# Attention on one core: the next head's context keys projected in the second unit of a head instead of the first, and one PSUM bank for all projection groups

## The chip, the cores and the metric

The kernel runs on one core of a Trainium2 chip. The metric is device time in microseconds (us) of one execution, the median of several runs. TensorE (PE in the profile, its weight loads PEld) multiplies, VectorE (DVE), ScalarE (ACT) and GpSimd (POOL) do the elementwise work, and every transfer is issued from one queue, SyncE's (SP).

## The reference, cut to what matters

Two trunk layers over 1024 latent tokens and 256 context tokens of width 1024. Layer 0 has differential attention with 8 heads, layer 1 a state-space mixer; an MLP follows each. The change touches layer 0's attention alone:

```python
def diff_attention(h_lat, h_ctx, w_qkv, ...):
    q_l, k_l, v_l = split(h_lat @ w_qkv)           # 8 heads, two 64-wide components each
    q_l, k_l = rope(q_l) * scale, rope(k_l)
    k_c, v_c = split(h_ctx @ w_qkv[:, QK_COLS:])   # context keys: no rotary
    k_all, v_all = concat([k_c, k_l]), concat([v_c, v_l])      # 256 + 1024 tokens
    def attend(q, k, v):
        p = softmax(q @ k.T)                       # one softmax for each component
        w = p[:, :, 0] - lam * p[:, :, 1]
        return rmsnorm(w @ v, subln_g) * (1 - lambda_init)
```

The context's own queries attend to the 256 context keys, the latent queries to all 1280.

## The kernel before, in words

The attention is the loop over `n` at the end of `phase_b`. A head `h` has nine units. Unit 0 takes the two query tiles of the context (256 keys), units 1 to 8 one latent query tile of 128 each (1280 keys). In a unit, `scores` multiplies queries with keys into PSUM (line 516 in unit 0, line 522 later), `maxima` has DVE copy the scores out with their row extremes (lines 531 and 535), `exps` has ACT exponentiate (lines 542 and 545), and `combine` has DVE subtract the two softmaxes (lines 553 to 556). A unit's result is transposed in the next unit: `w_part` has TensorE transpose it in up to three parts (line 568; 563 for unit 0's result, which has one part) into bank 5, a half of bank 6, or bank 7, and `w_evac` brings it to SBUF as a high and a low part: the first part through ACT and DVE (lines 576 and 577), the others through ACT and POOL (lines 581 to 583). In the units that have an output to make (`pv`; unit 2 for the context pair, units 4, 6, 8 and the next head's unit 1 for the latent pairs), `values` multiplies these with the value rows into bank 6, and `pair_out` copies the sum out (line 664). Where an output of latent tokens is due, both evacuations of the parts 0 and 1 stand behind `combine`.

Each product of a projection or of `values` is three matmuls, high by high, high by low, low by high (`mm3`, lines 132 to 134).

Between this work the projections of the next head's keys and queries are spread: `proj_group(h + 1, T, g, ...)`, with `T` 1 for keys and 0 for queries, and `g` 2 for the 256 context tokens, 0 and 1 for the halves of the latent tokens. A group is eight products, 24 matmuls. The groups of the latent tokens end in `evac` (ACT line 468, DVE line 469, four small DMAs that swap halves), `sine` (POOL line 474), `add` (DVE line 477) and `store` (ACT line 137, DVE line 138 into the buffer `stg`, then the DMAs Kd<-R or Qd<-R to DRAM). The context group of the keys has no rotary: `direct` (ACT line 463, DVE line 464) writes `stg` at once, and two DMAs Kd<-R take it out. There is one `stg`. The steps after the first are queued in `post` and taken one at a time by `next_post`, two a unit.

The table `AHEAD` gives the groups of each unit. In unit 0 there are two: the keys' context group (1, 2) in bank 4, all of it right behind `scores`, and the keys' first half (1, 0) in bank 7, in three pieces between the transposes. Units 2, 3, 5 and 7 have one group each, in bank 7; the others have none. Scores take banks 0 to 4 (0 and 1 in unit 0).

The loop stands in a manual schedule, so PE, DVE, ACT and POOL run in the order in which the code is written. SP's queue isn't part of it: a scheduler places the transfers, and SP issues them strictly one after the other, so a transfer that waits holds up those behind it. The names in the order's rows: R_111 is the buffer of weights, queries, values and `stg`, R_1826 the keys, F_1827 the scores, W weights and tables, FC the rotary buffers, Kd, Qd, Vd, od, on and rsd lie in DRAM.

Of the kernel before, what the change touches and what calls it, by code (L numbers as in the profile page):

```python
# [70 lines left out]
class Prog:  # L71
# [64 lines left out]
    def split(self, hi, lo, src, lo_eng=None):  # L136
        self.nc.scalar.activation(hi, src, AF.Copy)  # L137
        (lo_eng or self.nc.vector).tensor_tensor(lo, src, hi.bitcast(F32), ALU.subtract)  # L138
# [301 lines left out]

        return split

    def proj_group(self, h, T, g, wt, bank=None):

        nc = self.nc
        n, c0 = self.G_TOK[g], (256, 768, 0)[g]
        b = (self.qb.next() if bank is None else bank)[:, 0:n]
        scale = 1.0 if T else -0.125
        t = slice(c0 - 256, c0 + 256)
        hT = self.hT[g]  # L450
        q, sw, qc, s = self.rq, self.rs, self.rc, self.stg[:, :, 0:n]

        def product(k):
            return lambda: self.mm3(b, wt[k][0], wt[k][1], hT[0][:, k], hT[1][:, k], k == 0, k == 7)

        def out():
            dst = self.Kd if T else self.Qd
            for c in range(2):
                self.dma(dst[h % 2, c, :, c0 : c0 + n].rearrange("(l r) n -> r l n", l=2),
                         s[64 * c : 64 * c + 64].bitcast(F32))  # L460

        def direct():
            nc.scalar.activation(s[:, 0], b, AF.Copy, scale=scale)
            nc.vector.scalar_tensor_tensor(s[:, 1], b, scale, s[:, 0].bitcast(F32), ALU.mult, ALU.subtract)
            out()

        def evac():
            nc.scalar.activation(q, b, AF.Copy, scale=scale)
            nc.vector.scalar_tensor_tensor(qc, b, scale, self.cosT[:, t], ALU.mult, ALU.mult)
            for j in range(4):  # L470
                self.dma(sw[32 * j : 32 * j + 32], q[32 * (j ^ 1) : 32 * (j ^ 1) + 32])

        def sine():
            nc.gpsimd.tensor_tensor(sw, sw, self.sinT[:, t], ALU.mult)

        def add():
            nc.vector.tensor_tensor(qc, qc, sw, ALU.add)

        def store():
            self.split(s[:, 0], s[:, 1], qc)  # L480
            out()

        return [product(k) for k in range(8)], [direct] if g == 2 else [evac, None, sine, add, store]
# [103 lines left out]
        return self.tc.manual_schedule(engines={nc.tensor.engine, nc.vector.engine, nc.scalar.engine, nc.gpsimd.engine})  # L587


    AHEAD = {0: ((1, 2), (1, 0)), 2: ((1, 1),), 3: ((0, 2),), 5: ((0, 0),), 7: ((0, 1),)}  # L590

    def b_start(self):

# [25 lines left out]
    def phase_b(self):  # L619
# [14 lines left out]
        def load_k(h, c):  # L634
            K = loaded[h, "k", c] = self.rv(0, 1280) if (h, c) == (7, 1) else Kr.next()
            for k0, k1 in ((0, 256), (256, 1280)):
                self.dma(K[:, k0:k1].bitcast(F32), self.Kd[h % 2, c, :, k0:k1])

        def load_v(h):
            V = loaded[h, "v"] = Vr.next(), Vr.next()  # L640
            for j in range(2):
                self.dma(V[j].bitcast(F32), self.Vd[h, j])

        def load_q(h, pair):
            Q = Qr.next()
            cols = slice(256 * pair, 256 * pair + 256)
            self.dma(Q[:, :, 0].bitcast(F32), self.Qd[h % 2, :, :, cols].rearrange("c r n -> r c n"))
            for hl in range(2):
                self.dma(Q[64 * hl : 64 * hl + 64, :, 1].bitcast(F32),
                         self.Qd[h % 2, :, 64 - 64 * hl : 128 - 64 * hl, cols].rearrange("c r n -> r c n"))  # L650
            loaded[h, pair] = Q
# [122 lines left out]
        def wo_group(i):  # L774
            g = 2 if i > 7 else i // 4
            c0 = 128 * (i - self.G_TILES[g][0])
            b = self.bank(i - 6 if 6 < i < 8 else 7)

            def product(k):
                hh, hl = (t[:, k, c0 : c0 + 128] for t in self.oT[g])  # L780
                return lambda: self.mm3(b, hh, hl, wt6[k][0], wt6[k][1], k == 0, k == 5)

            def out():
                wsum = wsums.next()
                nc.scalar.activation(wsum, b, AF.Copy)
                self.dma(self.wod[i], wsum)

            return [product(k) for k in range(6)], [out]
# [13 lines left out]
        wts = {1: split(1)}  # L802

        def next_post():
            f = post.pop(0) if post else None
            if f:
                f()
# [3 lines left out]
        def evac():  # L811
            while ready:
                self.w_evac(*ready.pop(0))

        with self.manual():
            for n in range(72 + 5):
                h, u = units[n] if n < 72 else (8, 9)
                front = n < 72
                groups = []
# [7 lines left out]
                if front:  # L827
                    K = loaded[h, 'k', 0], loaded[h, 'k', 1]
                    pair = (u + 1) // 2
                    Q = loaded[h, pair]  # L830
                    s0 = hst[:, 0, h]
                    p, sn, sm = (p0.next(), p1), self.stat.next(), self.stat.next()
                    if u == 5 and h < 7:
                        load_v(h + 1)
                        load_k(h + 1, 0)
                    if u % 2 == 0 and u < 8 and (h, pair + 1) not in loaded:
                        load_q(h, pair + 1)
                    if h < 7:
                        groups = [self.proj_group(h + 1, *a, wts[a[0]], self.bank(4) if a == (1, 2) else None)
                                  for a in self.AHEAD.get(u, ())]  # L840
                    self.scores(u, Q, K)
                    if len(groups) == 2:
                        for f in groups[0][0]:
                            f()
                    if u == 8 and h < 7:
                        load_k(h + 1, 1)
                        load_q(h + 1, 0)
                        load_q(h + 1, 1)
                    self.maxima(u, p, sm)
                    if len(groups) == 2:  # L850
                        groups[0][1][0]()
                if front:
                    if h < 7:
                        if u == 0:
# [3 lines left out]
                if 65 <= n < 75:  # L858
                    groups = [wo_group(wo_order[n - 65])]
                fills = [[], [], []]  # L860
                if h >= 7 and groups:
                    fills = [groups[0][0][i : i + 2] for i in (0, 2, 4)]
                elif groups:
                    fills = [groups[-1][0][i:j] for i, j in (((0, 4), (4, 8), (8, 8)) if u == 3 else ((0, 3), (3, 6), (6, 8)))]
                if pv:
                    values(*pv)
                for part in range(3):
                    if part < parts:
                        tb = pb[:, 256:512] if part == 1 else self.bank(7 if part == 2 and not groups else 5)
                        t = self.w_part(prev[1], prev[2], part, tb)  # L870
                        ready.append((*t, part == 0))
                    if not late or part == 2:
                        evac()
                    if part == 1:
                        next_post()
                    if front and part < 2:
                        self.exps(u, part, p, sm, s0, sn)
                    if front and part == 1:
                        if n - 7 >= 9 and (n - 7) % 9 < 5 and (n - 7) // 9 < 7:
                            norm_pair((n - 7) // 9 - 1, (n - 7) % 9)  # L880
                        self.combine(u, p, s0, sn)
                    if late and part == 1:
                        evac()
                    if part == 0:
                        todo7, run7 = run7, []
                        for f in todo7:
                            f.pop(0)()
                            if f:
                                run7.append(f)
                    if part == (2 if n < 73 else 0):  # L890
                        while sums and sums[0][0] <= n:
                            sums.pop(0)[1]()
                    for f in fills[part]:
                        f()
                if pv:
                    pair_out(*pv)
                    sums.append((n + 1, lambda a=pv: pair_sums(*a)))
                    if pv[0] == 7:
                        tail.append((n + 1, pv[1]))
                next_post()  # L900
                if groups:
                    rest = groups[-1][1]
                    rest[0]()
                    post += rest[1:]
                if h < 7 and u in (0, 2):
# [1564 lines left out]
```

## Time and profile before

| | |
|---|---|
| median of 3 runs | 2883.9 us (2876.67 to 2889.97) |
| profiled execution, its own time | 2889.5 us |
| its span, first to last instruction | 2887.7 us |
| mean granted TensorE clock | 0.985 |
| busy share of the span: PE, PEld, DVE, ACT, POOL | 95%, 79%, 70%, 47%, 35% |
| attention loop | about 220 to 866 us of the span; PE busy 605.29 of 646.00 us |
| a head | about 80 us (unit 0 of heads 2 and 3 starts at 371.46 and 451.20 us) |

A row of the timeline has start, duration, engine, line, operation, what it writes and reads, shapes and count; in brackets stands how long the engine was idle before it and what ended that. A row of the chain of waits' table has who waited for whom, the sum in us, the number of waits and the longest. Heads are counted from 0 to 7; head 7 has no next head and no projection groups.

### The profile page before, as it was taken

To read this page: it belongs to the slowest core of one execution; us is meant where nothing else is said; L and a number is where in the kernel's file an instruction comes from. 1 tells how busy PE (TensorE), PEld (TensorE's weight loads), DVE (VectorE), ACT (ScalarE), POOL (GpSimd) and SP (SyncE) were. 2 spreads that over 40 slices of the span, in tenths; PEclk is the share of its full clock that TensorE was granted. 3 is DMA by queue.
4 is the path that set the end of the run, shared out by engine and by line. 5 is a ranking of instruction groups with operands and counts; after the bars stand their busy time and mean duration, and the time that the engine had idled before them with its cause. 6 is when DMAs were issued, how large, how long until landed. Compare 5 with 4: busy or idle time off the path is not lost. (4 is left out here: it accounts for less than half of the span.)

```text
span 2887.7 us, 43592 instructions
## 1 busy us (share of the span) xinstructions
PE 2738.5 (95%) x15225; PEld 2288.3 (79%) x15225; DVE 2009.4 (70%) x2968; ACT 1361.9 (47%) x2551; POOL 1016.2 (35%) x899
## 2 busy tenths in 40 slices
PE   6999999999999999999999999789899999999999
PEld 4687888888877888778877778688788777888887
DVE  5456788778873676666788768799533597768466
ACT  3425555555654743323444435477443633344443
POOL 3314666666663600000020003588120243336314
PEclk9999999999999999999999999899899999999999
DMA  9955555555736458886799887479843144467544
GB/s 299 306 172 168 152 173 170 171 163 165 252 98 185 123 197 311 280 298 214 261 292 294 263 251 246 155 230 279 261 135 106 63 162 164 157 222 245 164 131 142
DMA packets 447785, 586.33 MB, mean 203 GB/s; under 512 B 60494, under 2 KB 293196, under 8 KB 444364
## 3 DMA queue, kind: packets, MB, share of 16 engines
q1 hardware_dynamic: 447564, 583.53, 63.6%
q8 instruction: 120, 1.97, 0.3%
q14 instruction: 101, 0.83, 0.1%
HBM read 396.38 MB, written 182.82 MB: 201 GB/s over the span
## 5 line engine op out<-in xcount | busy, mean ns | idle before, releaser
L132 PE MATMUL PS<-H 128*128 128x512 f32 x1056 | 415.7, 395 | 7.5 <-DVE FD L1622 5.0
L134 PE MATMUL PS<-H 128*128 128x512 f32 x1056 | 412.6, 391 | 3.1 <-DVE H L138 1.6
L133 PE MATMUL PS<-H 128*128 128x512 f32 x1056 | 413.8, 392 | 0.0
L132 PE MATMUL PS<-H,R 128*128 128x512 f32 (+1 forms) x828 | 308.8, 375 | 4.7 <-DVE FU L1545 1.7
L133 PE MATMUL PS<-H,R 128*128 128x512 f32 (+1 forms) x828 | 299.7, 362 | 1.4 <-POOL H L138 1.4
L134 PE MATMUL PS<-H,R 128*128 128x512 f32 (+1 forms) x828 | 298.9, 362 | 0.0
L132 PEld LDWEIGHTS PS<-H 128*128 128x128 f32 x1056 | 199.1, 189 | 54.1 <-DVE FD L1622 4.9
L134 PEld LDWEIGHTS PS<-H 128*128 128x128 f32 x1056 | 199.2, 189 | 46.5 <-DVE H L138 2.6
L133 PEld LDWEIGHTS PS<-H 128*128 128x128 f32 x1056 | 199.2, 189 | 40.9 <-issue 1.0
L545 ACT ACTIVATE F<-F,stat 128x1280 f32<-128x1280 f32 x128 | 174.3, 1362 | 100.4 <-DVE F L535 100.2
L132 PE MATMUL PS<-R,H 128*128 128x512 f32 x536 | 214.6, 403 | 1.6 <-ACT R L137 1.6
L133 PE MATMUL PS<-R,H 128*128 128x512 f32 x536 | 211.6, 395 | 0.2 <-POOL R L138 0.2
L134 PE MATMUL PS<-R,H 128*128 128x512 f32 x536 | 209.7, 395 | 1.8 <-DVE H L138 1.8
L137 ACT ACTIVATE R<-W 128x512 fp32r<-128x512 f32 (+1 forms) x186 | 130.6, 711 | 170.9 <-PE PS L133 101.1
L137 ACT ACTIVATE H<-U 128x640 fp32r<-128x640 f32 x216 | 132.6, 677 | 148.5 <-PE PS L133 105.3
L138 DVE TENSOR_TENSOR H<-W,H 128x512 fp32r<-128x512 f32 (+1 forms) x137 | 123.4, 911 | 103.2 <-ACT H L137 102.5
L138 DVE TENSOR_TENSOR H<-U,H 128x640 fp32r<-128x640 f32 x216 | 165.8, 803 | 37.7 <-ACT H L137 37.6
L535 DVE TENSOR_SCALAR_CACHE_REDUCE F<-PS 128x1280 f32<-128x1280 f32 x128 | 185.2, 1483 | 7.6 <-PE PS L522 7.3
L137 ACT ACTIVATE H<-W 128x512 fp32r<-128x512 f32 (+2 forms) x158 | 95.7, 613 | 192.6 <-PE PS L133 114.5
L132 PEld LDWEIGHTS PS<-H,R 128*128 128x128 f32 x828 | 158.5, 192 | 30.4 <-issue 4.1
L134 PEld LDWEIGHTS PS<-H,R 128*128 128x128 f32 x828 | 158.2, 191 | 25.5 <-issue 0.8
L582 POOL TENSOR_SCALAR R<-F 128x256 fp32r<-128x256 f32 (+1 forms) x128 | 126.8, 991 | 146.5 <-ACT F L581 128.7
(514 smaller groups left out, 6827.2 us busy)
## 6 DMA issues: line engine op xcount, KB each, us to landing
W<-in_mlp_w SPq DMA_DIRECT2D x176, 256.0 KB, 3.0
U<-Aa SPq DMA_DIRECT2D x108, 320.0 KB, 4.4
Aa<-FU SPq DMA_DIRECT2D x91, 320.0 KB, 4.6
Ad<-F SPq DMA_DIRECT2D x112, 256.0 KB, 3.0
W<-Ad SPq DMA_DIRECT2D x112, 256.0 KB, 2.7
FU<-in_mlp_w SPq DMA_DIRECT2D x32, 512.0 KB, 5.9
Ta<-FU SPq DMA_DIRECT2D x16, 1024.0 KB, 4.0
recd<-U SPq DMA_DIRECT2D x64, 256.0 KB, 4.3
```

The source lines that it names most:

```text
L132: mm(out, ah, bh, start=first, stop=False, **kw)
L133: mm(out, ah, bl, start=False, stop=False, **kw)
L134: mm(out, al, bh, start=False, stop=last, **kw)
L137: self.nc.scalar.activation(hi, src, AF.Copy)
L138: (lo_eng or self.nc.vector).tensor_tensor(lo, src, hi.bitcast(F32), ALU.subtract)
L535: ts(p[c], self.PS[:, 1280 * c : 1280 * c + 1280], 1.0, None, ALU.mult, ALU.min, accum_out=sm[:, c : c + 1])
L545: nc.scalar.activation(p[c], p[c], AF.Exp, bias=sm[:, c : c + 1], scale=-1.0, accum_out=sn[:, 0:1] if c else s0[:, u + 1 : u + 2])
L582: nc.gpsimd.tensor_scalar(hi, t, 1.0, 0.0, ALU.mult, ALU.add)
```

## The change

The context group (1, 2) moves from unit 0 to unit 1 and uses bank 7, as every other group of the loop. In unit 1 its eight products stand behind `values` and the transposes, four in the second and four in the third part of the unit (`FILLS`). Its `direct` moves from behind unit 0's `maxima` to the end of unit 1. An added call of `next_post` in unit 0 stands right before another one.

```diff
-    def proj_group(self, h, T, g, wt, bank=None):
+    def proj_group(self, h, T, g, wt):
...
-        b = (self.qb.next() if bank is None else bank)[:, 0:n]
+        b = self.qb.next()[:, 0:n]
...
-    AHEAD = {0: ((1, 2), (1, 0)), 2: ((1, 1),), 3: ((0, 2),), 5: ((0, 0),), 7: ((0, 1),)}
+    AHEAD = {0: (1, 0), 1: (1, 2), 2: (1, 1), 3: (0, 2), 5: (0, 0), 7: (0, 1)}
+    FILLS = {1: (0, 0, 4, 8), 3: (0, 4, 8, 8)}
...
-                        groups = [self.proj_group(h + 1, *a, wts[a[0]], self.bank(4) if a == (1, 2) else None)
-                                  for a in self.AHEAD.get(u, ())]
+                        groups = [self.proj_group(h + 1, *a, wts[a[0]]) for a in (self.AHEAD[u],)] if u in self.AHEAD else []
                     self.scores(u, Q, K)
-                    if len(groups) == 2:
-                        for f in groups[0][0]:
-                            f()
...
                     self.maxima(u, p, sm)
-                    if len(groups) == 2:
-                        groups[0][1][0]()
...
-                    fills = [groups[-1][0][i:j] for i, j in (((0, 4), (4, 8), (8, 8)) if u == 3 else ((0, 3), (3, 6), (6, 8)))]
+                    a = self.FILLS.get(u, (0, 3, 6, 8))
+                    fills = [groups[0][0][a[i] : a[i + 1]] for i in range(3)]
...
                     for f in fills[part]:
                         f()
+                if front and u == 0:
+                    next_post()
                 if pv:
                     pair_out(*pv)
...
-                    rest = groups[-1][1]
+                    rest = groups[0][1]
```

What the change moves is seen in the order of the instructions on three engines. First PE, at the start of unit 0 of head 2. Before, the context group's matmuls (H are the tokens, 256 wide) follow the eight scores:

```order
L568 MATMUL PS<-ident,F_1827 128x128 x10
L516 MATMUL PS<-R_1826,R_111 128x256 x8
L132 MATMUL PS<-H,R_111 128x256
L133 MATMUL PS<-H,R_111 128x256
L134 MATMUL PS<-H,R_111 128x256
```

Now the transposes of the unit before follow, and then the 512 wide group:

```order
L568 MATMUL PS<-ident,F_1827 128x128 x10
L516 MATMUL PS<-R_1826,R_111 128x256 x8
L568 MATMUL PS<-ident,F_1827 128x128 x4
L132 MATMUL PS<-H,R_111 128x512
L133 MATMUL PS<-H,R_111 128x512
L134 MATMUL PS<-H,R_111 128x512
```

The 24 matmuls went one unit later, to between line 563 and the scores of unit 2; nothing else moved on PE in the attention. Second DVE, from the end of unit 1 to the start of unit 2 of the same head. Before:

```order
L556 SCALAR_TENSOR_TENSOR F_1827<-F_1827,stat 128x1280
L577 TENSOR_TENSOR R_111<-PS,R_111 128x512
L535 TENSOR_SCALAR F_1827,stat<-PS 128x1280 x2
L577 TENSOR_TENSOR R_111<-PS,R_111 128x4x128
L477 TENSOR_TENSOR FC<-FC 128x512
```

And now, with line 464 (the context group's evacuation) ahead of unit 2's maxima:

```order
L556 SCALAR_TENSOR_TENSOR F_1827<-F_1827,stat 128x1280
L577 TENSOR_TENSOR R_111<-PS,R_111 128x512
L464 SCALAR_TENSOR_TENSOR R_111<-PS,R_111 128x256
L535 TENSOR_SCALAR F_1827,stat<-PS 128x1280 x2
L577 TENSOR_TENSOR R_111<-PS,R_111 128x4x128
```

Line 464 left its place between unit 0's maxima (line 531) and line 577. Third SP, in units 0 and 1 of the same head. Before, the context keys' two stores stand among the loads of queries, and a load of the just stored 256 keys follows ahead of the norm's traffic, the store Qd<-R and the four swaps FC<-FC:

```order
L80 DMA R_111<-Qd 128x2x256
L80 DMA R_111<-Qd 64x2x256
L80 DMA Kd<-R_111 64x2x256 x2
L80 DMA R_111<-Qd 64x2x256
L80 DMA F_1827<-rsd 128x256
L80 DMA R_1826<-Kd 128x256
L80 DMA on<-F_1827 128x256 x2
L80 DMA F_1827<-od 128x256
L80 DMA Qd<-R_111 64x2x512 x2
L80 DMA FC<-FC 32x512 x4
```

Now stores and load stand behind all of these and behind the value loads, at the end of unit 1 and the start of unit 2:

```order
L80 DMA Qd<-R_111 64x2x512 x2
L80 DMA FC<-FC 32x512 x4
L80 DMA R_111<-Vd 128x1280 x2
L80 DMA on<-W 128x256
L80 DMA od<-FC 128x256
L80 DMA on<-W 128x256
L80 DMA W<-od 128x256
L80 DMA Kd<-R_111 64x2x256 x2
L80 DMA R_111<-Qd 128x2x256
L80 DMA R_111<-Qd 64x2x256 x2
L80 DMA R_1826<-Kd 128x256
```

Nothing between the swaps of unit 0 and the value loads is new; the two stores and the load moved behind them.

## Prediction

> **What bounds the kernel now.** I read the page first, then the waits of the attention loop, then the timeline of one head (head 2) on each engine.
>
> ```profile
> PE 2738.5 (95%) x15225; PEld 2288.3 (79%) x15225; DVE 2009.4 (70%) x2968; ACT 1361.9 (47%) x2551; POOL 1016.2 (35%) x899
> ```
>
> PE is the bound. The change adds and removes no work on it (24 matmuls move), so the time can change only by PE's idle time. The waits between 230 and 900 us show where that lies:
>
> ```profile
> PE PS L568 <- DVE R L577: 11.2, 9, 2.0
> ACT R L137 <- DMA Kd<-R: 11.1, 5, 3.3
> PE PS L516 <- DMA R<-Kd: 9.5, 6, 2.1
> PE PS L133 <- DVE R L577: 8.9, 6, 1.6
> PE PS L132 <- ACT FC L664: 1.5, 3, 1.0
> ```
>
> PE waits some 31 us in these four rows, for transposes (L568), for unit 0's scores (L516) and for the value product's first matmuls (L132, L133). One wait is ACT's own: `store` (L137) writes `stg` and must wait until the context keys' DMA has read it. To see how these hang together, PE in units 0 to 2 and 5 of head 2:
>
> ```profile
> 373.59 0.98 PE L516 MATMUL PS<-R,R 128*128 128x256 f32 x6 [1.65 <-DMA R<-Kd]
> 374.40 0.28 PE L132 MATMUL PS<-H,R 128*128 128x256 f32 x1
> ...
> 377.28 0.60 PE L568 MATMUL PS<-ident,F 128*128 128x128 f32 x4
> ...
> 384.36 2.49 PE L522 MATMUL PS<-R,R 128*128 128x512 f32 x12
> ...
> 390.63 2.57 PE L522 MATMUL PS<-R,R 128*128 128x512 f32 x12
> 393.39 0.38 PE L132 MATMUL PS<-R 128*128 128x256 f32 x1 [0.20 <-ACT FC L664]
> 395.40 0.38 PE L133 MATMUL PS<-R 128*128 128x256 f32 x1 [1.63 <-DVE R L577]
> ...
> 396.46 0.48 PE L132 MATMUL PS<-H,R 128*128 128x512 f32 x1
> ...
> 420.63 0.66 PE L568 MATMUL PS<-ident,F 128*128 128x128 f32 x4 [1.20 <-DVE R L577]
> ```
>
> The context group runs from 374.40 to 377.28, that is 2.88 us; the transposes of unit 8's result follow without a wait. Unit 1 (from 384.36) has scores, 30 matmuls of `values` and one part of transposes, and unit 2 begins at 390.63, only 6.27 us later. There PE stalls: the value product needs the low part of what unit 1 transposed. DVE in the same stretch:
>
> ```profile
> 374.59 0.68 DVE L577 TENSOR_TENSOR R<-PS,R 128x512 fp32r<-128x512 f32 x1
> ...
> 383.39 0.48 DVE L556 SCALAR_TENSOR_TENSOR F<-F,stat 128x256 f32<-128x256 f32 x1
> 386.42 0.69 DVE L138 TENSOR_TENSOR R<-FC,R 128x512 fp32r<-128x512 f32 x1 [2.54 <-ACT R L137]
> 387.22 0.69 DVE L469 SCALAR_TENSOR_TENSOR FC<-PS,W 128x512 f32<-128x512 f32 x1
> 387.83 1.48 DVE L535 TENSOR_SCALAR_CACHE_REDUCE F<-PS 128x1280 f32<-128x1280 f32 x1
> ...
> 394.67 0.68 DVE L577 TENSOR_TENSOR R<-PS,R 128x512 fp32r<-128x512 f32 x1
> ```
>
> And ACT's wait with the transfers behind it:
>
> ```profile
> 385.75 0.63 ACT L137 ACTIVATE R<-FC 128x512 fp32r<-128x512 f32 x1 [2.29 <-DMA Kd<-R]
> ```
>
> ```profile
> 367.13 1.27 SPq L80 DMA_DIRECT2D Qd<-R  x2
> ...
> 379.09 1.27 SPq L80 DMA_DIRECT2D Kd<-R  x2
> ```
>
> So the chain is: the context keys' store is issued at 379.09 and holds `stg` until about 385.7; ACT's L137 waits for it, DVE's L138 for that (2.54 us), and unit 1's maxima begin only at 387.83, though scores of unit 1 stood in PSUM from about 385.6 (the first half of the row at 384.36). From there to the end of L577, 395.35, DVE and ACT need 7.5 us (maxima, two exponentials, `combine`), and PE waits for that end.
>
> **The change part by part.**
>
> *What comes late in unit 0 (a cost).* With the context group gone, the transposes that started at 377.28 could start at 374.40. They go to bank 5, which L577 empties at 374.59 + 0.68 = 375.27. So a wait appears that the group has hidden: 0.87 us, and some 0.06 for the signal (the L577 at 394.67 ends at 395.35, and PE goes on at 395.40). The size differs by head:
>
> ```profile
> 296.94 0.28 PE L132 MATMUL PS<-H,R 128*128 128x256 f32 x1
> ```
>
> ```profile
> 296.74 0.68 DVE L577 TENSOR_TENSOR R<-PS,R 128x512 fp32r<-128x512 f32 x1
> ```
>
> ```profile
> 454.59 0.28 PE L132 MATMUL PS<-H,R 128*128 128x256 f32 x1
> ```
>
> ```profile
> 454.27 0.68 DVE L577 TENSOR_TENSOR R<-PS,R 128x512 fp32r<-128x512 f32 x1
> ```
>
> Head 1: 297.42 - 296.94 = 0.48. Head 3: 454.95 - 454.59 = 0.36. Heads 4 to 6 are taken like head 2. Head 0 has no unit before it. Sum: 0.48 + 0.36 + 4 x 0.87, with 0.06 six times, **+4.7 us**. Its bounds: nothing (the scores' wait for the keys, 1.65 us, could grow and cover it), and 1.60 in each of six heads, 9.6 us, from head 7, whose unit 0 has no group at all:
>
> ```profile
> 778.07 1.31 PE L568 MATMUL PS<-ident,F 128*128 128x128 f32 x10 [1.60 <-DVE R L577]
> ```
>
> I keep to the heads' own rows, since head 7's keys came without a wait and so left L577 less time.
>
> *What goes in unit 2 (a gain).* PE does everything of unit 0 after that wait earlier by 2.88 - 0.93 = 1.95 us, and the 24 matmuls then lengthen unit 1 by 2.88: unit 2's scores start 0.93 later than before, at 391.56, and its value product could start at 394.1 (393.39 without the 0.20, plus 0.93). On the other side `store` finds `stg` free: the transfer before it is the Qd<-R of 367.13. L138 then follows `combine`'s end at 383.87, and L469 ends two steps of 0.69 later, by about 385.3, so unit 1's maxima start some 2.5 us earlier (387.83 - 385.3; the scores are there from 383.6, PE being 1.95 earlier), and L577 ends near 392.9, 1.2 before PE asks for it. The wait is gone with 1.2 us to spare; half of the 2.5 would do. ACT's L664, the 0.20, has the same cover of 2.88 us of context matmuls.
>
> What this is worth: 8.9 us in six waits by the table, of which head 7, with no group, keeps its own,
>
> ```profile
> 797.05 0.39 PE L133 MATMUL PS<-R 128*128 128x256 f32 x1 [1.19 <-DVE R L577]
> ```
>
> leaves 7.7 in heads 2 to 6; 1.5 for L664; and 0.26 for each of the five, since the matmul before a wait lasts 0.38 where the next one usually starts 0.12 after it (the rows at 393.39 and 374.40 against 24 in 2.88): 7.7 + 1.5 + 1.3 = **-10.5 us**. Bounds: 0 (the waits stay) and, if unit 5's wait (below) shrinks too, -19. Head 1 has no such wait, so there its 0.5 is all cost.
>
> *Head 0* waits where unit 2 transposes:
>
> ```profile
> 241.63 0.66 PE L568 MATMUL PS<-ident,F 128*128 128x128 f32 x4 [1.40 <-DVE F L556]
> ```
>
> Unit 1's scores come 2.88 us sooner and with them maxima and `combine`; PE arrives at the same time. I take the whole **-1.4**, bounds 0 and -1.4.
>
> *L463 and L464* move with the group. L464, some 0.4 us by L469's 0.69 for twice the columns, now stands ahead of unit 2's maxima. It waits for the last context matmul, 391.5, and for ACT, so it ends by 393.3, right behind L577; unit 2's scores are half done at 392.9. Unit 2's maxima start at 393.4 instead of 395.3. Cost nothing; if L577 were as late as today, 0.4 in each head.
>
> *One bank.* The context group's first matmul in unit 1 needs bank 7 free: L469 ended at 387.91 even before, PE comes at 388.7. The first key product of unit 2 (396.46, now some 395.2) needs L464's end, 393.3. Covers of 0.8 and 1.9 us, so no cost.
>
> *SP.* The two stores of keys now wait for L464 behind the value loads. Behind them stand queries and keys that are needed two units later or more. In unit 0 the queue loses a blockage. No cost; what hangs on the store's landing is the next `store`, at the end of unit 2, which came at
>
> ```profile
> 402.36 0.65 ACT L137 ACTIVATE R<-FC 128x512 fp32r<-128x512 f32 x1
> ```
>
> Issued at 393.4 and landing after the 6.6 us that it took in unit 0 (379.09 to 385.7), it frees `stg` at 400.0, 1.1 before the moved L137 (402.36 - 1.3).
>
> *The added `next_post`* takes the store, which the call right behind took before: nothing moves. Behind the attention a handful of instructions changed places with their neighbours; taken at 0, bounds of 2 us either way (the largest wait in the table is 2.1).
>
> **Sum.** +4.7 - 10.5 - 1.4 = -7.2 us. The profiled execution has 2889.5 us beside a span of 2887.7; it would take 2882.3. It lies 5.6 above the median of 2883.9, so against the median: 2876.7, say **2877**, 0.24% faster. About 0.5% (14.4 us) is what a measurement of this kernel can tell from no change; its own three runs spread over 13.3 us.
>
> **The rivals.**
>
> *A, the waits only move.* DVE and ACT need 7.5 us from maxima to L577, and head 7 waits 1.19 at the same place though nothing held its `stg`. If unit 1's maxima stay at 387.83 for another reason (POOL's `sine`, ahead of `add` and `combine`), L577 ends at 395.35 as before, PE is held to the same moment, and only head 1 pays: 2884. Against it: head 7 has no context matmuls in unit 1, which cover 2.88 us.
>
> *B, slower: the one bank and what DVE does for it.* Every group must now be emptied before the next begins, and L464 stands in front of unit 2's maxima. If L577 of unit 1 ends later than about 394.5 (so that L464 ends behind PE's transposes of unit 2), then L464's 0.4 delays the maxima and all that hangs on them in seven heads, ACT's L463 (taken at the same 0.4) goes with it, and unit 2's waits stay as long as today: 7 x 0.8 = +5.6 and head 1's 0.5, 2890. For the slower side by more than 0.5% unit 0's waits would have to be head 7's 1.60 as well (+9.6): 2899. [...] The trace speaks against it here: between two groups of bank 7 PE has scores, values and transposes to do, and the covers above are 0.8 and 1.9 us.
>
> *C, more than forecast.* PE's wait in unit 5 (1.20 at 420.63) ends with DVE, too, and DVE would be 1.9 us ahead in unit 2 where PE is 1.3 ahead. If the difference lasts to unit 5, or all of its wait goes: 7 x 1.2 = 8.4 more, 2869. Against it: DVE in units 3 and 4 follows PE's matmuls again.
>
> **How the numbers follow.** Forecast 0.56 (its own range 2870 to 2884, from the covers and the runs' spread), A 0.14, B 0.17, C 0.13. The range runs from C's middle less a few us for the spread to B: 2866 to 2891. Faster by over 0.5% (under 2869.5): half of C and the low end of the forecast, 0.12. Slower by over 0.5% (over 2898.3): B's upper end, 0.07. Within: 0.81.
>
> **What would show it.** In the changed profile: unit 0's transposes (L568) wait 0.3 to 1.0 us for L577 in heads 1 to 6; ACT's wait on DMA Kd<-R is gone or small; L133's wait for L577 is left in head 7 alone; L516's wait for the keys stays near 1.6 a head; unit 5's wait stays near 1.2. I am wrong if L133's waits stay (A), if L568 or the first context matmul waits for L464 or L469 (B), or if ACT's wait on Kd<-R comes back at the end of unit 2.

## The result, and the profile after

The changed kernel takes 2872.6 us (median of 20 runs, 2864.74 to 2878.39) beside 2881.0 us for the kernel before (20 runs on the same chip, 2867.31 to 2890.21). The ratio is 0.9975, 95% interval 0.9965 to 0.9984: 7.2 us less, between 4.6 and 10.1 (the two medians lie 8.4 apart). The profiled execution takes 2870.1 us with a span of 2868.3 us. The gain was foreseen at its size, 7.2 us, and it comes from where the prediction put it. The forecast time of 2877 us is 4 us too high, mostly because it stands on a median of three executions, 2883.9 us, which lies 2.9 above that of the 20.

The page's first row: PE does the same work, and DVE and POOL are a little busier than before (2009.4 and 1016.2 us).

```profile
PE 2730.3 (95%) x15225; PEld 2281.8 (80%) x15225; DVE 2016.2 (70%) x2968; ACT 1363.1 (48%) x2551; POOL 1021.6 (36%) x899
```

PE's waits between 230 and 900 us (who waits, for whom; us in all, times, the longest):

```profile
PE PS L568 <- DVE R L577: 14.5, 15, 2.0
PE PS L516 <- DMA R<-Kd: 9.8, 6, 2.1
...
PE PS L133 <- DVE R L577: 1.2, 1, 1.2
PE PS L132 <- ACT FC L665: 0.9, 1, 0.9
```

The transposes' wait for L577 grew by 3.3 us (11.2 before), the keys' wait is nearly as it was (9.5), and the value product's wait for L577 fell from 8.9 to head 7's 1.2. The ACT row for Kd<-R (11.1 us before) is gone from the table, and so is head 0's 1.40. Here is PE in units 0, 2 and 5 of head 2 (lines from 588 on stand one higher than before: L664 is now L665):

```profile
372.83 0.97 PE L516 MATMUL PS<-R,R 128*128 128x256 f32 x6 [1.71 <-DMA R<-Kd]
374.51 0.66 PE L568 MATMUL PS<-ident,F 128*128 128x128 f32 x4 [0.70 <-DVE R L577]
...
387.90 0.36 PE L132 MATMUL PS<-H,R 128*128 128x256 f32 x1
...
390.86 2.49 PE L522 MATMUL PS<-R,R 128*128 128x512 f32 x12
393.19 0.28 PE L132 MATMUL PS<-R 128*128 128x256 f32 x1
393.31 0.28 PE L133 MATMUL PS<-R 128*128 128x256 f32 x1
...
394.26 0.48 PE L132 MATMUL PS<-H,R 128*128 128x512 f32 x1
...
418.44 0.66 PE L568 MATMUL PS<-ident,F 128*128 128x128 f32 x4 [1.20 <-DVE R L577]
```

The new wait stands in unit 0 (0.70), the context group now starts at 387.90 in unit 1, and in unit 2 the value product follows the scores without a stop. Unit 5 waits its 1.20 as before. DVE in the same stretch, and what POOL does beside it:

```profile
382.74 1.78 DVE L138 TENSOR_TENSOR R<-FC,R 128x512 fp32r<-128x512 f32 x1
384.63 0.69 DVE L469 SCALAR_TENSOR_TENSOR FC<-PS,W 128x512 f32<-128x512 f32 x1
385.24 1.48 DVE L535 TENSOR_SCALAR_CACHE_REDUCE F<-PS 128x1280 f32<-128x1280 f32 x1
...
392.09 0.68 DVE L577 TENSOR_TENSOR R<-PS,R 128x512 fp32r<-128x512 f32 x1
392.69 0.41 DVE L464 SCALAR_TENSOR_TENSOR R<-PS,R 128x256 fp32r<-128x256 f32 x1
393.02 1.48 DVE L535 TENSOR_SCALAR_CACHE_REDUCE F<-PS 128x1280 f32<-128x1280 f32 x1
```

```profile
382.63 1.34 POOL L583 TENSOR_TENSOR R<-F,R 128x512 fp32r<-128x512 f32 x1
384.05 1.64 POOL L138 TENSOR_TENSOR R<-W,R 128x512 fp32r<-128x512 f32 x1
```

DVE's wait of 2.54 us ahead of L138 is gone. The head itself starts 0.82 us earlier in this profile (its first scores at 370.64, before at 371.46), so the two profiles are compared from there: unit 1's maxima start 14.60 us into the head, before 16.37, that is 1.8 us earlier. L577 ends at 392.77, 0.42 us ahead of PE's value product.

### The profile page after: what moved, and what is told of

It reads as the page before. It is cut to its first block, busy times and chain, and to the rows that moved or that the text cites. A ratio compares the mean times of both kernels' runs of the same rounds, so it can differ in the third digit from the quotient of the medians.

```text
span 2868.3 us, 43597 instructions
## 1 busy us (share of the span) xinstructions
PE 2730.3 (95%) x15225; PEld 2281.8 (80%) x15225; DVE 2016.2 (70%) x2968; ACT 1363.1 (48%) x2551; POOL 1021.6 (36%) x899
## 5 line engine op out<-in xcount | busy, mean ns | idle before, releaser
L132 PE MATMUL PS<-H 128*128 128x512 f32 x1056 | 416.0, 395 | 8.6 <-DVE FD L1620 5.7
L133 PE MATMUL PS<-H 128*128 128x512 f32 x1056 | 414.8, 393 | 0.0
L132 PE MATMUL PS<-H,R 128*128 128x512 f32 (+1 forms) x828 | 307.5, 374 | 3.6 <-ACT R L137 1.6
L133 PE MATMUL PS<-H,R 128*128 128x512 f32 (+1 forms) x828 | 298.2, 360 | 1.4 <-POOL H L138 1.4
L132 PEld LDWEIGHTS PS<-H 128*128 128x128 f32 x1056 | 199.4, 189 | 55.0 <-issue 6.4
L133 PEld LDWEIGHTS PS<-H 128*128 128x128 f32 x1056 | 199.7, 189 | 41.5 <-issue 1.0
L132 PE MATMUL PS<-R,H 128*128 128x512 f32 x536 | 213.6, 401 | 1.4 <-ACT R L137 1.4
L137 ACT ACTIVATE R<-W 128x512 fp32r<-128x512 f32 (+1 forms) x186 | 130.8, 712 | 172.3 <-PE PS L133 99.2
L133 PE MATMUL PS<-R,H 128*128 128x512 f32 x536 | 210.9, 394 | 0.0
L137 ACT ACTIVATE H<-U 128x640 fp32r<-128x640 f32 x216 | 132.9, 678 | 150.9 <-PE PS L133 104.5
L138 DVE TENSOR_TENSOR H<-W,H 128x512 fp32r<-128x512 f32 (+1 forms) x137 | 124.2, 917 | 103.8 <-ACT H L137 103.1
L138 DVE TENSOR_TENSOR H<-U,H 128x640 fp32r<-128x640 f32 x216 | 165.9, 805 | 39.7 <-ACT H L137 37.8
L137 ACT ACTIVATE H<-W 128x512 fp32r<-128x512 f32 (+2 forms) x158 | 96.1, 616 | 191.2 <-PE PS L133 114.3
L132 PEld LDWEIGHTS PS<-H,R 128*128 128x128 f32 x828 | 156.8, 190 | 29.7 <-issue 4.1
```

What stands on the lines that cost most here:

```text
L132: mm(out, ah, bh, start=first, stop=False, **kw)
L133: mm(out, ah, bl, start=False, stop=False, **kw)
```

## A second effect: stretches of half clock

The two profiles differ by more than the waits. Heads 2 to 6 before (head 5 is the row of 81.10), then heads 2 and 6 after, the three between them lasting 78.3 to 78.4 at the same clock; each from the first scores of its unit 0 to those of the next head (length, then busy time of each engine, granted clock, DMA share and GB/s):

```profile
371.50:451.20 79.70, 75.03 (x481) 66.48 (x480) 64.44 (x101) 46.80 (x96) 53.05 (x51) 1.00 0.56 167
451.20:532.10 80.90, 76.34 (x483) 68.04 (x481) 64.72 (x101) 46.80 (x96) 53.00 (x51) 0.98 0.56 165
532.10:614.30 82.20, 76.87 (x481) 67.78 (x480) 64.46 (x101) 46.73 (x96) 52.83 (x51) 0.98 0.55 162
614.30:695.40 81.10, 76.66 (x482) 67.74 (x481) 64.44 (x101) 46.80 (x96) 52.93 (x51) 0.98 0.56 165
695.40:775.30 79.90, 75.08 (x483) 66.55 (x481) 63.17 (x103) 46.98 (x97) 50.49 (x49) 1.00 0.78 236
```

```profile
370.64:449.05 78.41, 74.79 (x482) 66.54 (x481) 65.61 (x101) 46.95 (x96) 53.55 (x51) 1.00 0.58 170
...
684.04:762.45 78.41, 74.80 (x482) 66.55 (x480) 64.84 (x103) 47.09 (x97) 51.21 (x50) 1.00 0.80 246
```

Before, heads 2 and 6 have the full clock and last 79.7 and 79.9 us; heads 3 to 5 show 0.98 and last 1.1 to 2.4 us more. After, each of these five heads has the full clock and lasts 78.3 to 78.4. So heads of full clock differ by 1.4 us on average, about what the waits are worth (the prediction's terms, 10.5 less 4.1 in five heads, give 1.3 for each). The five heads together fell by 12.0 us (403.8 to 391.8). Of these, 7.2 are five times the 1.44 between the means of the heads of full clock (79.80 and 78.36), and the other 4.8 are the three slow heads. What happens in them is seen in head 5 before, behind unit 2's wait:

```profile
638.07 0.38 PE L133 MATMUL PS<-R 128*128 128x256 f32 x1 [1.63 <-DVE R L577]
...
639.12 0.73 PE L132 MATMUL PS<-H,R 128*128 128x512 f32 x1
639.64 0.63 PE L133 MATMUL PS<-H,R 128*128 128x512 f32 x1
...
642.20 0.58 PE L133 MATMUL PS<-H,R 128*128 128x512 f32 x1
642.62 0.40 PE L134 MATMUL PS<-H,R 128*128 128x512 f32 x1
```

```profile
636.00:643.00 7.00, 5.37 (x23) 4.30 (x22) 6.43 (x9) 1.94 (x4) 3.12 (x3) 0.76 0.96 318
```

The 512 wide matmuls start 0.43 us apart instead of 0.23, and from 642.62 on they are back at 0.40 long. The granted clock is 0.50 from 639.20 to 642.50, which is the half clock of the heading and makes the 0.76 of these 7 us. So here a wait was paid twice, once as 1.63 us of idle time and once as slow matmuls behind it; that the one brings the other is argued here from their order alone and examined below, under busy_wait. The prediction counts only the idle time.

## The experiments

Theories: **the buffer** (the context keys' store held `stg`; once it does not, unit 2's wait goes, whatever PE has in front of it) against **the cover** (24 more matmuls in unit 1 hide the chain); **one bank** costs or does not; and, for what is left, **the waits move** against **they go**. Each timed kernel stands against the kernel before on the same chip.

**own_stg.** The kernel before, with a 2 KB buffer of its own for the context group's evacuation.

```diff
+        if g == 2 and self.own is not None:
+            s = self.own
...
+        self.own = self.view(self.R1, 20, (2, 256))
```

> The kernel before, with the context keys' evacuation in a 2 KB buffer of its own instead of the shared stg; nothing else differs. Theory (the held stg made unit 1's maxima late, and that was PE's wait in unit 2): ACT's wait on DMA Kd<-R goes, unit 1's maxima start some 2.5 us earlier, L577 ends near PE's need, and the 10.5 us of waits in unit 2 fall below 2, while unit 0's transposes stay covered: 8 to 10 us faster than before, ratio 0.9965 to 0.9972, even a little faster than the change. Rival (the 24 matmuls that fill unit 1 are the whole gain, the stg wait lay beside the path): L133's waits stay at 1.6 in heads 2 to 6, ratio 0.9995 to 1.0005.

Measured: 2870.4 us beside 2880.5, ratio 0.9964 (0.9948 to 0.9980). PE's waits (lines shifted by two) and a head:

```profile
PE PS L518 <- DMA R<-Kd: 10.0, 6, 2.2
...
PE PS L133 <- DVE R L579: 2.4, 6, 1.2
```

```profile
529.60:607.50 77.90, 74.76 (x480) 66.48 (x479) 64.76 (x101) 46.85 (x96) 53.02 (x51) 1.00 0.57 171
```

The buffer alone gives what the change gives (the intervals overlap), with all 24 matmuls still in unit 0, and keeps unit 0's cover. The 0.23 us a head that is left in unit 2 shows what the missing cover there costs. The order of the transfers is that of the kernel before: the stores at 381.24, the load that waits for them at 386.62 and the swaps behind it at 390.91. So it wasn't the held-up queue either. The held buffer was the cause.

**second_store.** The changed kernel, with the buffer held again: in unit 0 a dummy evacuation of the same size into `stg`, stored to spare DRAM.

```diff
+                    if u == 0 and h < 7:
+                        src, s = self.PS[:, 0:256], self.stg[:, :, 0:256]
+                        nc.scalar.activation(s[:, 0], src, AF.Copy)
+                        nc.vector.scalar_tensor_tensor(s[:, 1], src, 1.0, s[:, 0].bitcast(F32), ALU.mult, ALU.subtract)
+                        for c in range(2):
+                            self.dma(self.spare[h % 2, c, :, 0:256].rearrange("(l r) n -> r l n", l=2),
+                                     s[64 * c : 64 * c + 64].bitcast(F32))
```

> The changed kernel, with the suspected wait put back: behind unit 0's maxima a second evacuation like the context keys' (from a bank of scores, into stg, two DMAs to a spare DRAM tensor that nobody reads). PE's order stays that of the changed kernel. Theory (both are needed: PE's cover of 2.88 us is about as long as the delay): ACT's L137 waits 1.5 to 2.3 us again, L577 of unit 1 ends near 395.3 on head 2's clock and PE asks near 394.1, so L133 waits about 1.2 us again in heads 2 to 6; 6 to 8 us lost, ratio to the kernel before 0.999 to 1.001. Rival (the cover alone is the gain): L133 waits only in head 7, ratio 0.9975 to 0.9985.

Measured: 2877.5 us, ratio 0.9996 (0.9980 to 1.0011): the gain is lost, and the interval barely touches the change's. ACT's and PE's waits, and heads 2 and 3:

```profile
ACT R L137 <- DMA spare<-R: 14.3, 6, 3.6
```

```profile
PE PS L133 <- DVE R L577: 3.3, 4, 1.3
```

```profile
369.20:448.80 79.60, 76.01 (x481) 67.55 (x479) 64.64 (x102) 47.18 (x97) 52.98 (x51) 0.98 0.57 169
448.80:528.80 80.00, 75.10 (x483) 66.60 (x481) 65.08 (x102) 47.02 (x97) 53.23 (x51) 1.00 0.59 172
```

ACT waits for the store again. Unit 2's wait is shorter than before the change (the cover of 24 matmuls takes part of it): 0.3 to 1.3 us in three of the five heads, where 1.2 in all five were expected. It is missing where a stretch of half clock has made PE late, in heads 2 and 4 (granted clock 0.98 in both). The dummy is also work of its own, some 0.4 us on ACT and on DVE in each head by the rows of lines 463 and 464, and the run does not tell this apart from the wait. The cover alone isn't the gain.

**bank6.** The changed kernel, its context group in a free half of bank 6 instead of bank 7.

```diff
+        b = self.qb.next()[:, 0:n] if bank is None else bank
...
+                        groups = [self.proj_group(h + 1, *a, wts[a[0]], pb[:, 256:512] if u == 1 else None) for a in (self.AHEAD[u],)] if u in self.AHEAD else []
```

> The changed kernel, with a bank of its own again for the context group: the free half of bank 6 in unit 1, so that its matmuls and the key groups of units 0 and 2 wait for no common bank. Theory (no wait hangs on the one bank: in the changed profile bank 7 is emptied 2.5 us before the context group and 1.1 us before unit 2's keys need it): no change against the changed kernel, ratio to the kernel before 0.997 to 0.998, no wait on L464 or L469 to lose. Rival (sharing costs an overlap): 2 to 5 us faster than the change, ratio 0.996 or less.

Measured: 2871.5 us beside 2877.6, ratio 0.9978 (0.9964 to 0.9993); the change has 0.9975. No gain from a bank of its own is seen.

**change_own.** The change and the buffer together.

```diff
+        if g == 2 and self.own is not None:
+            s = self.own
```

> The changed kernel, with the separate evacuation buffer of the run own_stg. Theory (once moved, the context group meets a free stg): nothing left to gain, ratio to the kernel before 0.997 to 0.998. Rival (stg still holds something up at the end of unit 1 or 2): ratio 0.9965 or less, with ACT's L137 or L463 starting earlier.

Measured: 2871.0 us beside 2877.6, ratio 0.9968 (0.9955 to 0.9980). The ratio lies between the forecast (0.997 to 0.998) and the rival's bound (0.9965), and the interval overlaps the change's for the most part, so the times do not decide. Its profile has the change's waits and none of ACT for a store, and half clock again in head 2 where the changed kernel's own profile has none:

```profile
371.50:451.40 79.90, 76.31 (x481) 67.70 (x480) 64.81 (x101) 46.93 (x96) 52.89 (x51) 0.98 0.57 167
```

So the change does not do away with these stretches; it leaves fewer waits that can be followed by one.

**fill0.** The changed kernel, with unit 0's first three products (9 matmuls) ahead of the first transposes instead of behind them, which covers the new wait.

```diff
+                    if part == 0 and h < 7 and u in (0,):
+                        for f in fills[0]:
+                            f()
+                        fills[0] = []
                     if part < parts:
```

> The changed kernel, with the first three products of unit 0's group ahead of the first transposes instead of behind them: 2.1 us of PE work in the place of the cover that the change took away. Theory (unit 0's new waits are real cost on the path): L568's waits of 0.2 to 0.7 us in unit 0 of heads 1 to 6 go, 3.4 us by the changed kernel's profile, ratio to the kernel before about 0.9963. Rival (the wait comes back in unit 1 or 2, since the transposes and all behind them are 1.4 us later): ratio 0.9975.

Measured: 2868.3 us beside 2880.5, ratio 0.9960 (0.9947 to 0.9974). Unit 0's waits for L577 are gone, and the ratio is the expected one, though its interval overlaps the change's; a quarter of a microsecond comes back in unit 2 of four heads:

```profile
PE PS L568 <- DVE R L577: 11.4, 9, 2.0
...
PE PS L133 <- DVE R L577: 2.2, 5, 1.2
```

**fill05** does the same in unit 5 (`u in (0, 5)`).

> As the run before, and the same in unit 5, where the transposes wait 1.2 us for L577 in every head. Theory (PE's wait there is covered like unit 0's, DVE being ahead afterwards): 6 to 7 heads by 1.2, so another 8 us, ratio to the kernel before about 0.994. Rival (DVE and ACT are the bound in units 4 to 8, and the wait moves to unit 6 or to unit 0): ratio 0.996 as without it.

Measured: 2868.4 us beside 2880.5, ratio 0.9955 (0.9936 to 0.9974), nearer the rival's 0.996 than the 0.994 of the theory. The wait of 1.20 in unit 5 has become one of 0.76 in front of the next transposes:

```profile
421.70 0.66 PE L568 MATMUL PS<-ident,F 128*128 128x128 f32 x4 [0.76 <-DVE R L577]
```

**fill05b** puts five products instead of three between unit 5's first and second transposes.

```diff
-    FILLS = {1: (0, 0, 4, 8), 3: (0, 4, 8, 8)}
+    FILLS = {1: (0, 0, 4, 8), 3: (0, 4, 8, 8), 5: (0, 3, 8, 8)}
```

> The run fill05 with unit 5's eight products in pieces of 3, 5 and 0 instead of 3, 3 and 2. In fill05 the wait of 1.2 us at unit 5's first transposes had become one of 0.77 at its third, which use the same bank 5 again and so wait for the first part's L577. Theory: two products more ahead of them, 1.4 us, cover that: 0.77 in seven heads, 5 us, ratio to the kernel before about 0.9935 against 0.9955 (the idle time of PE in heads 1 to 6 falls to about 2.0 us). Rival (it moves on to unit 6): ratio as fill05.

Measured: 2869.5 us beside 2877.6, ratio 0.9967 (0.9955 to 0.9978): missed. The 0.76 went, but waits elsewhere grew, among them that for the keys (2.47 us in head 3, a head with a granted clock of 0.98). Over its 12 executions the mean granted clock is 0.9857, beside 0.9868 of the kernel before. By estimate (0.0011 of 2870 us) that is at most 3 of the some 9 us by which it missed; the rest was not resolved. PE's waits, and heads 2 and 3:

```profile
PE PS L516 <- DMA R<-Kd: 12.0, 6, 2.5
...
PE PS L691 <- ACT FC L673: 3.3, 6, 0.6
```

```profile
368.90:446.30 77.40, 74.61 (x482) 66.59 (x480) 65.53 (x101) 46.52 (x96) 53.97 (x51) 1.00 0.59 171
446.30:525.10 78.80, 75.78 (x483) 67.88 (x480) 65.09 (x101) 46.56 (x96) 53.77 (x51) 0.98 0.58 170
```

**own_fill5b.** own_stg with fill05b's order in unit 5.

```diff
-(((0, 4), (4, 8), (8, 8)) if u == 3 else ((0, 3), (3, 6), (6, 8)))
+(((0, 4), (4, 8), (8, 8)) if u == 3 else ((0, 3), (3, 8), (8, 8)) if u == 5 else ((0, 3), (3, 6), (6, 8)))
...
+                    if part == 0 and h < 7 and u in (5,):
+                        for f in fills[0]:
+                            f()
+                        fills[0] = []
```

> The kernel before with the separate buffer of own_stg, the context group left in unit 0 and bank 4, and unit 5's products in pieces of 3 (ahead of the transposes), 5 and 0. Theory: own_stg's gain of 0.36% and unit 5's 1.2 us in seven heads, 8 us: ratio about 0.9935, the same as fill05b, so that where the context group stands matters no more once nothing waits for stg and something covers unit 0. Rival: the moved group is worth something by itself, and fill05b is faster by 3 us or more.

Measured: 2872.7 us beside 2877.6, ratio 0.9984 (0.9972 to 0.9996): missed in the same way (mean granted clock 0.9856). fill05b is faster by 3.2 us, which is the rival's mark, but the two intervals overlap. Here head 0's wait of 1.4 us and unit 2's 0.23 in five heads are left, which come to most of it, so that the moved group is worth more than that is not shown.

```profile
PE PS L518 <- DMA R<-Kd: 12.0, 6, 2.7
```

**busy_wait** tests whether the idle time of PE itself brings the half clock. The kernel before, with 13 dummy matmuls where unit 2 waits:

```diff
+                if u == 2 and 2 <= h <= 6:
+                    for _ in range(13):
+                        mm(self.bank(7)[:, 0:256], loaded[h, "v"][0][:, 0], K[0][:, 0:256], start=True, stop=True)
                 if pv:
                     values(*pv)
```

> The kernel before, with 13 dummy matmuls (a 128x256 product of values and keys into bank 7, never read; 13 x 0.12 = 1.56 us) ahead of unit 2's value product in heads 2 to 6, where PE waits 1.27 to 2.57 us. Theory (an idle PE of some 1.6 us is charged twice: once as the wait, once as a stretch of half clock that follows it in some heads): the dummies take the place of the wait, so no time is added, L133's waits fall to a total under 3 us, no half-clock stretch follows unit 2 in heads 2 to 6, and those heads last 79.2 to 80.0 us (before: 79.74, 80.89, 82.25, 81.06, 79.86); ratio 0.998 to 1.000. Rival (the longer heads have another cause, or the dummies only push the chain back): heads 4 and 5 stay over 81 us, or all five grow by 1.5 us; ratio 1.000 to 1.003.

Measured: 2879.7 us beside 2877.8, ratio 0.9999 (0.9985 to 1.0012). Head 5 in unit 2, and heads 2 and 5 as a whole:

```profile
636.50 1.71 PE L867 MATMUL PS<-R,R 128*128 128x256 f32 x13
638.05 0.28 PE L132 MATMUL PS<-R 128*128 128x256 f32 x1
...
639.12 0.48 PE L132 MATMUL PS<-H,R 128*128 128x512 f32 x1
```

```profile
375.00:454.30 79.30, 76.35 (x494) 68.10 (x492) 64.43 (x101) 46.76 (x96) 52.95 (x51) 1.00 0.56 168
...
613.00:693.90 80.90, 77.62 (x496) 69.62 (x493) 64.70 (x101) 46.73 (x96) 52.94 (x51) 0.98 0.55 165
```

The dummies fit into the wait, and no half clock follows unit 2 in any of the five heads: four of them have a granted clock of 1.00, and in head 5, with 0.98, the 512 wide matmuls behind unit 2 start 0.23 us apart (639.44, 639.67, 639.90). The waits for the keys were left in (10.3 us in six, the longest 2.4). The times (0.9999) show no gain.

The length of a wait alone does not tell here whether half clock follows it. Before, heads 2 to 6 have nine waits of PE between 1.57 and 2.09 us, in unit 0 for the keys and in unit 2 for L577, and three of them were followed by a granted clock of 0.50 or 0.51: 2.09 us in head 3 (from 454.86 to 458.30), 1.61 in head 4 (557.20 to 560.70) and 1.63 in head 5. The other six were not: 1.65 and 1.63 in head 2, 1.57 in head 4, 1.60 in head 5, 1.71 and 1.62 in head 6. Heads 2 and 5 have a wait of the same 1.63 us at the same place, and only head 5 slows down behind it. After, the same heads have one such wait each, for the keys (1.71, 2.14, 1.66, 1.70 and 1.68 us), and none was followed by it. The DMA share does not tell the two cases apart either: it is 0.96 around unit 2's wait in head 5 before, with half clock, and 1.00 in head 2 (393 to 400), without. So no stretch is seen in unit 2 where the dummies cover its wait, but what decides which wait is followed by one was not shown, and one profile by itself is weak evidence.

**early_k** takes away the wait for the keys: the 256 context columns of the second component's keys get two buffers of their own and are loaded in unit 5 of the head before.

```diff
-            for k0, k1 in ((0, 256), (256, 1280)):
+            for k0, k1 in ((0, 256), (256, 1280))[c:]:
...
+        Kc = Ring([self.view(self.R1, 20 + i, (256,)) for i in range(2)])
+        def load_kc(h):
+            loaded[h, "kc"] = Kc.next()
+            self.dma(loaded[h, "kc"].bitcast(F32), self.Kd[h % 2, 1, :, 0:256])
```

> The changed kernel, with the 256 context columns of the second component's keys in two 1 KB buffers of their own, loaded at unit 5 of the head before instead of at its unit 8; all else as in the change. L516's wait for the keys (1.66 to 2.14 us in heads 2 to 6) goes. Theory (unit 0's transposes are held by DVE's L577, whose time does not hang on the keys): the wait for L577 grows by the same amount, to 2.3 us, heads stay at 78.0 to 78.4 us, ratio 0.996 to 0.998. Rival (L577 comes earlier too, since DVE's work before it waits for PE): heads 76.7 to 77.2 us, ratio 0.993 to 0.994.

Measured: 2877.4 us beside 2877.8, ratio 0.9989 (0.9974 to 1.0005), above the 0.996 to 0.998 expected. The waits' sum is nearly what it was (25.6 for 14.5 and 9.8), in one place now; heads 2 and 3:

```profile
PE PS L568 <- DVE R L577: 25.6, 15, 2.6
```

```profile
370.70:450.60 79.90, 76.06 (x482) 67.78 (x480) 64.64 (x101) 46.91 (x96) 52.65 (x51) 0.98 0.56 166
450.60:528.90 78.30, 74.50 (x481) 66.47 (x480) 65.63 (x101) 46.72 (x96) 53.57 (x51) 1.00 0.58 172
```

A clean head takes 78.3 us, as in the change: the keys are not what holds unit 0, DVE is. One wait of 2.6 us in place of 1.7 and 0.7 gains nothing. Why the median is slightly worse stays open: the interval overlaps the change's, and the mean granted clock over the executions, 0.9870 beside the change's 0.9872, does not explain it.

**early_k6** adds to that six of unit 0's eight products ahead of its transposes (`FILLS` 0: (0, 6, 8, 8)).

> As early_k, and the first six of unit 0's eight products (18 matmuls, 2.16 us) ahead of unit 0's first transposes instead of behind them. Theory: neither the keys nor L577 is waited for over 0.3 us in unit 0, heads 2 to 6 last 76.4 to 77.0 us (78.3 in the change), no half-clock stretch in heads 1 to 6, ratio 0.992 to 0.994. Rival (the wait only goes on to unit 2, where DVE and ACT end L577 too late by what PE has gained): L133's wait comes back with 1 to 2 us a head, heads 77.7 to 78.4 us, ratio 0.996 to 0.998.

Measured: 2872.9 us beside 2877.8, ratio 0.9975 (0.9960 to 0.9990). The 18 matmuls are 512 wide and start 0.23 us apart, so they take 4.1 us and not the 2.16 of the expectation. The rival holds: heads are at 78.1 us, and the waits have gone on to the projection's start (for ACT's L581) and to unit 2.

```profile
PE PS L133 <- DVE R L577: 8.7, 7, 3.8
PE PS L132 <- ACT F L581: 5.6, 5, 1.1
```

Undisturbed heads take 77.4 to 78.5 us in every version in which the buffer is free. A wait that is covered reappears, often smaller, at the next place that hangs on DVE and ACT. The best of these, fill0 and fill05, beat the kernel before by 0.40 and 0.45%. Their undisturbed heads are 0.4 and 0.8 us shorter than the change's, but the intervals of their ratios overlap the change's, so the times do not show that they are faster than it.

## Why the prediction was right

*The waits in unit 2.* Forecast -10.5, of which 7.7 for L133, 1.5 for L664 and 1.3 for the slow first matmul. L133's wait fell by exactly 7.7. The L132 row lost all of its 1.5 in heads 2 to 6, and head 7 has a new 0.9, which the forecast lacks. PE's busy time in heads 2 and 6 fell by 0.24 and 0.28 us, as the 0.26 for the slow first matmul says. The cause was the one named: own_stg takes away only the buffer's wait and gains as much, second_store brings the wait back and loses the gain. Rival A falls: nothing else held the maxima at 387.83.

*Its margin.* This is the term that came out worst. L577 was to end 1.2 us ahead of PE, it ended 0.42 ahead. The step that failed is "L469 ends two steps of 0.69 later": in heads 2 to 6 alike L138 took 1.78 us in its new place, where POOL's L583 runs at the same time (382.63 to 383.97). So unit 1's maxima came 1.8 us earlier and not 2.5. The profile before already had such a row: L138 takes 1.09 us at 403.14, beside POOL. Without the 24 matmuls in unit 1 PE would have come before L577's end, and a wait would be left, as own_stg's 0.23 is.

*Unit 0's cost.* Forecast +4.7; the table's row grew by 3.3 us. In head 2 the wait is 0.70 where 0.93 was forecast. The bound of 9.6 was not needed. Head 1, where the forecast sees 0.5 of cost and no gain, lasts 77.1 us after and 76.7 before. fill0 shows the cost was real: covering it takes off some 0.4 us of a head's 78.4.

*Head 0's 1.4* went, as taken. *Unit 5's wait* stayed at 1.20, so rival C falls.

*One bank, L464.* L464 ended at 393.10, ahead of the first key product at 394.26 (cover 1.2, forecast 1.9), and unit 2's maxima began at 393.02, which is 393.8 on the prediction's clock (0.82 later), where the forecast is 393.4. L577 ended at 393.6 on that clock, so B's condition, later than 394.5, was missed by 0.9 us. With a bank of its own for the group, bank6 has 0.9978 where the change has 0.9975.

*SP.* The stores of the keys go out at 393.12, and the next L137 (400.16) does not wait for them: no cost, as taken.

*The sum.* -7.2 by the terms, -7.2 by the ratio. That the two agree so well is partly luck: the interval is 4.6 to 10.1 us, unit 0 cost 1.4 less than forecast, head 7 has its new 0.9, and the half clock, which the sum lacks, adds to the gain in some executions and not in others. Over many executions it adds little: the mean granted clock is 0.9872 in the change's 20, and 0.9865 to 0.9868 in three sets of 24 to 35 of the kernel before, by estimate 1 to 2 us of 2880 at the most. The two profiled executions overstate it. They differ by 19.4 us: 12.0 in heads 2 to 6, of which 4.8 are half clock; most of the other 7.4 lies behind head 6, where the change moves next to nothing. Their granted clocks, 0.985 and 0.989, account by estimate (0.004 of 2880) for at most 11.5 of the 19.4.

## What to carry to other kernels

Where a transfer out of a staging buffer stands in front of the next write to it, follow that write to the engine behind it: here a store's 6.6 us reached PE through ACT, DVE, the maxima and L577, and either 2 KB or another place for the store took the wait away. Moving work to make room uncovers what it hid, so look at both ends; and when several waits hang on one chain of DVE and ACT, covering one of them brings up the next. Check first whether an operation takes longer beside its new neighbour on another engine, as L138 did here (1.78 us instead of 0.69).

## What the runs showed of the hardware

*Half clock after short waits.* In head 5 before, a wait of 1.63 us was followed by matmuls at a granted clock of 0.50 (639.20 to 642.50). Of nine waits of 1.57 to 2.09 us in heads 2 to 6 before, three were followed by such a stretch and six were not; after, five of 1.66 to 2.14 us were followed by none. What decides was not shown. Between heads of one run a stretch goes with 1.0 to 1.6 us (79.10 against 78.10 in own_fill5b, 78.80 against 77.40 in fill05b, 79.90 against 78.30 in early_k).

*DVE beside POOL.* The same L138 takes 0.69 us where POOL is idle (386.42 before) and 1.78 us where POOL's L583 runs (382.74 after); it ends 0.55 us after L583 does, nearly as if it had begun only then. At 420.49 before, where L583 runs from 420.32 to 421.05, it takes 1.10 us and ends 0.54 us after it. L469 (FC<-PS,W) keeps its 0.69 at 384.63 beside POOL's L138 (384.05 to 385.69). That the one holds up the other is an inference from these rows; no run tests it by itself.
